# Up-projection of a fused encoder layer by seven block products, with the down-projection as a stage of its own

## The chip, the cores and the metric

One core of a Trainium2 chip runs the whole program. The metric is the device time of one execution in microseconds (us): the median of the runs. TensorE (PE) does the matmuls, VectorE (DVE), ScalarE (ACT) and GpSimd (POOL) work on tiles in the on-chip memory, SyncE (SP) starts most transfers. Matmuls accumulate in PSUM, in eight banks.

## What is computed

One step of an encoder layer on T = 1088 positions (1024 of a new stream, 64 of a running one), D = 1024 channels, float32. Cut to what matters here:

```python
hn = rmsnorm(x, g_pre1)
z = hn @ w_in
# ... gated linear recurrence (ya) and chunk-wise position mixing (yb) ...
mix = jnp.concatenate([ya, yb], axis=-1) @ w_o
x = x + rmsnorm(mix, g_post1)
hn2 = rmsnorm(x, g_pre2)
up = hn2 @ w_up
upc, new_ffn = causal_dwconv(up, ffn_prev, w_conv_f, b_conv_f)
f = (jax.nn.gelu(upc[..., :D_FF]) * upc[..., D_FF:]) @ w_down
x = x + rmsnorm(f, g_post2)
```

w_up is 1024 x 6144 (D_FF = 3072, a gate half and a value half), w_down 3072 x 1024. The convolution is over positions, three taps per channel.

## The kernel before, in words

All activations lie transposed: channels on the 128 partitions, positions along the row. A float32 matmul is done as three matmuls of a reduced format (fp32r): each operand is split into a high part (ScalarE copy, L122) and the rest (VectorE subtraction, L124 or L126), and high x high, high x low and low x high are added up in PSUM. So every product below counts three times.

The stages in order: the v projection (L268, L274), the tiles of the remaining input projection with the position mixing and the recurrence between them (L408, L489), the output projection `o_mm` (L626) in three chunks of positions (364, 364, 360), the code after it for each chunk, `post1`, then the up-projection with the down-projection between its parts, and the tail.

`post1` of a chunk runs beside the matmuls of the next one, piece by piece, as a generator that `o_mm` and `pre_up` step forward. It makes two norms. For each, `rstd_head` puts the sum of squares through TensorE (`st`, L179), VectorE (`v`, L170) and GpSimd (`rs`, a power, L171); `rstd_tail` spreads the result over the partitions with TensorE (`bp`, L191) and ScalarE copies it (`rr`, L193). Between them stand scaling (L682), residual addition (L683) and, in `add_sq`, squares on ScalarE (L201) and their sum (L202), which is on GpSimd for the first norm and for six of eight tiles of the second.

The up-projection has 24 pairs of tiles, a gate tile and a value tile of 128 channels each. The first two pairs (`pre_up`, L737) run chunk by chunk beside the last `post1`. Each other tile is `up_mm` (L721): 8 input tiles, 3 matmuls, 3 chunks, 72 matmuls. ScalarE copies the result out of PSUM (L725), VectorE convolves it in three passes (L762, L765), ScalarE applies GELU (L773), VectorE multiplies gate and value (L779) and the product is split into `gh` and `gl`. After every fourth pair `down` (L804) multiplies four finished pairs with their part of w_down, 288 matmuls, and adds to `facc` (L825, L827). The last group runs in column blocks of 284, 272, 272 and 260 (`last_down`) with the final norm between them.

What each engine does next is an order fixed when the program is built: instructions are queued as the code emits them, with `high_priority` moving a few ahead, and each engine takes its own queue in that order. Weights come by `prefetch`, one or two 512 KB loads ahead on SyncE, and are split when they are there. All larger tiles share one pool of 41 buffers (`NBIG`).

Of the kernel before, what the change touches and what calls it, by code (L numbers as in the profile page):

```python
# [18 lines left out]
GAP = 3  # L19
T = SEQ + DEC  # L20
# [11 lines left out]

LAST_COLS = [(0, 284), (284, 556), (556, 828), (828, 1088)]
LAST_ENG = ["gg", "vv", "vv", "gg", "vv", "vv", "vg", "vv"]
Y_STEPS = [(0,), (0, 0), (1, ), (2,), (1,), (1, 2), (2,), ()]
NPRE = 2
PRI = 120
NBIG = 41
# [17 lines left out]
def layer_kernel(ctx: ExitStack, tc, xT, w_fm, w_v, w_o, w_up, w_down, w_g, w_s, par, bc, yT, small, vn_out):  # L56
# [3 lines left out]
    quad = ctx.enter_context(tc.tile_pool(name="quad", bufs=1))  # L60
# [10 lines left out]
    def big_tile(dt=F32, shape=(P, 3 * CH), name="t"):  # L71
        return big.tile(list(shape), dt, tag="t", name=name)

    def tmp_tile(w, name="d"):
        return tmp.tile([P, NSB * P], F32, tag="d", name=name)[:, :w]

    def quad_tile(name):
        return quad.tile([P, 4, 3 * CH], F32, tag="q", name=name)
# [6 lines left out]

    def third(i, c):
        return slice(i % 3 * CH, i % 3 * CH + cw(c))
# [8 lines left out]
    def packed(n, dt, name, c):  # L96
        tiles = [big_tile(dt, name=name) for _ in range((n + 2) // 3)]
        return [tiles[i // 3][:, third(i, c)] for i in range(n)], tiles

    def v3(t, n, c):  # L100
        return t.rearrange("p (c t) -> p c t", c=3)[:, :n, :cw(c)]
# [30 lines left out]
    w_src.update({("up", i): w_up[i] for i in range(2 * NF)})  # L132
# [3 lines left out]
    for j in range(NF):  # L136
        order += [("up", 2 * j), ("up", 2 * j + 1)]
        if j % GRP == 0 and j:
            order += [("dn", j // GRP - 1, m) for m in range(4)]
    order += [("dn", NF // GRP - 1, m) for m in range(4)]  # L140
# [3 lines left out]
    shut = {"up"}  # L144
# [178 lines left out]
    s = quad_tile("s")  # L323
# [38 lines left out]
    def v_gate(b):  # L362
# [5 lines left out]
        for h in range(4):  # L368
            nc.vector.scalar_tensor_tensor(s[:, h, vcols(b)], sp[:, h, :n], pv("g_v", h), cc[:, h, :n],
                                           op0=ALU.mult, op1=ALU.add)  # L370
# [30 lines left out]
    def fm_mm(w, evac, fill=(), by_chunk=False):  # L401
        fill = list(fill)
        ps = [bank_tile("ps") for _ in range(3)]
        hi, lo = w

        def one(k, q, c):
            wt, at = ((hi, xh), (hi, xl), (lo, xh))[q]
            nc.tensor.matmul(ps[c][:, :cw(c)], wt[:, k * P:(k + 1) * P], at[k][:, cs(c)],  # L408
                             start=(k == 0 and q == 0), stop=(k == KD - 1 and q == 2))

        if by_chunk:
            for c in range(3):
                for k in range(KD):
                    for q in range(3):
                        one(k, q, c)
                evac(c, ps[c][:, :cw(c)])
        else:
            for k in range(KD):
                for q in range(3):
                    for c in range(3):  # L420
                        one(k, q, c)
# [6 lines left out]
            for c in range(3):  # L428
                evac(c, ps[c][:, :cw(c)])
# [86 lines left out]
    def u_tile(h, fill=()):  # L516
        sh = s[:, h, :T]
# [18 lines left out]
    def gate_tile_chunks(t, after):  # L536
# [3 lines left out]
        def evac(c, ps):  # L540
            nc.vector.tensor_tensor(g[:, cs(c)], ps, rb[c], op=ALU.mult)
            nc.scalar.activation(g[:, cs(c)], g[:, cs(c)], AF.Gelu_apprx_tanh)
            nc.vector.tensor_tensor(h[:, cs(c)], h[:, cs(c)], g[:, cs(c)], op=ALU.mult)
            sat3[c] = tmp_tile(cw(c), name="sat3")
            nc.scalar.activation(sat3[c], h[:, cs(c)], AF.Square)
            after(c)
# [20 lines left out]
    def slots(n, name):  # L567
        tiles = [None] * ((n + 2) // 3)

        def at(i, c):  # L570
            if tiles[i // 3] is None:
                tiles[i // 3] = big_tile(F32R, name=name)
            return tiles[i // 3][:, third(i, c)]

        return at

    yh, yl = {}, {}
    ysl = [slots(24, "yha"), slots(24, "yhb")]

    def y_split(c, half):  # L580
        head = rstd_head((sat if half == 0 else sbt)[:, cs(c)], DA, None if half else sat3[c])
        yield
        rr = tmp_tile(cw(c), name="rr")
        rstd_tail(head, rr)
        for i in range(4):
            k = half * 4 + i
            y = (hst[i] if half == 0 else s[:, i, :])[:, cs(c)]
            nc.vector.scalar_tensor_tensor(y, y, pv("g_out", k), rr, op0=ALU.mult, op1=ALU.mult)
            yh[k, c], yl[k, c] = ysl[half](c * 8 + 2 * i, c), ysl[half](c * 8 + 2 * i + 1, c)
# [12 lines left out]
    ys = [y_split(c, 1) for c in range(3)]  # L602
    for t in range(3):
        step(ys[t])
        gate_tile(t, [None, None, None, None, lambda: step(ys[t]), None, lambda: step(ys[t])])
    ys = [y_split(c, 0) for c in range(3)]
    gate_tile_chunks(3, lambda c: None)

# [3 lines left out]
    def o_mm(c, gen=iter(())):  # L612
        pss = {}

        def half_mm(mp, half, mi, first, last):
# [6 lines left out]
            ps = pss[m][:, :cw(c)]  # L622
            for i in range(4):
                k = half * 4 + i
                for j, (w, a) in enumerate(((hi, yh), (hi, yl), (lo, yh))):
                    nc.tensor.matmul(ps, w[:, i * 256 + mi * P:i * 256 + (mi + 1) * P], a[k, c],  # L626
                                     start=(first and i == 0 and j == 0), stop=(last and i == 3 and j == 2))

        if c == 1:
            q = quad_tile("mixq")  # L630
            mix = [q[:, i // 3, third(i, c)] for i in range(9)]
        else:
            mix, _ = packed(9, F32, "mix", c)
        ssq = mix.pop()

        def evac(m):
            nc.scalar.activation(mix[m], pss[m][:, :cw(c)], AF.Copy)
            add_sq(ssq, mix[m], m == 0, nc.gpsimd)

        if c == 0:  # L640
            for n, (mp, half) in enumerate(O_ORDER):
# [4 lines left out]
                for mi in range(2):  # L646
                    half_mm(mp, half, mi, half == 1, half == 0)
                    if half == 0:
                        evac(2 * mp + mi)
        else:  # L650
            for m in range(KD):
# [4 lines left out]
                if c == 2 and m % 2 == 1:  # L656
                    del wo[0, m // 2], wo[1, m // 2]
                    if m == 3:
                        shut.clear()
# [345 lines left out]
```

## Time and profile before

| what | value |
|---|---|
| time, median of 3 runs | 1251.18 us (1249.62 to 1251.53) |
| profiled execution: span from first to last instruction | 1244.9 us |
| median less that span | 6.3 us |
| TensorE busy, mean granted clock | 97%, 0.987 |
| VectorE, ScalarE, GpSimd busy | 53%, 32%, 11% |
| transferred | 75.50 MB, mean 61 GB/s |

The profile is of one execution of its own; the page gives its span, and the time around it is taken as the difference to the median. A share of busy time is a mean over stages with different limits, so a stage is read by itself: with the chain that ended last, the waits, and windows of the span. In the chain's lines "x24" counts the instructions of the piece; for statistics and broadcasts each matmul of the program shows as two there.

### The profile page before, as it was taken

The numbers are of one execution on the slowest core, as the hardware profiler recorded it, in microseconds if no ns is written. First come the engines' busy times: TensorE is split into PE (matmuls) and PEld (weight loads), VectorE is DVE, ScalarE is ACT, GpSimd is POOL, SyncE is SP. The second block draws the span as 40 slices with busy tenths as digits, with TensorE's granted clock in tenths as the row PEclk, the third lists the DMA queues.
The fourth block names the chain that finished last, engine by engine and source line by source line (L and its number), as shares of the span: only waits on it lengthen the run. The fifth ranks groups of instructions, "written<-read, shape, count | busy, mean of one in ns | idle before, by whom it ended". The sixth has DMA issues, their size and how long they took to land.

```text
span 1244.9 us, 17414 instructions
## 1 busy us (share of the span) xinstructions
PE 1210.9 (97%) x7334; PEld 1193.9 (96%) x7334; DVE 664.1 (53%) x958; ACT 392.5 (32%) x663; POOL 135.3 (11%) x233
## 2 busy tenths in 40 slices
PE   8998999998899999999999999999999999999995
PEld 6798999998899999999999999999999999999995
DVE  7585777655676755025542545425453353534676
ACT  7214656453443324222320222112320222112332
POOL 0213000034431000000000000000000000000045
PEclk9999999999998999999999999999999999999998
DMA  8110111211341112011111111211111111211323
GB/s 294 34 39 18 34 52 34 103 48 49 120 161 48 68 34 67 19 52 34 35 62 40 34 35 51 69 35 35 51 52 51 35 34 35 68 51 35 115 88 107
DMA packets 31421, 75.50 MB, mean 61 GB/s; under 512 B 2640, under 2 KB 17488, under 8 KB 31344
## 3 DMA queue, kind: packets, MB, share of 16 engines
q1 hardware_dynamic: 30672, 73.76, 17.7%
q8 instruction: 57, 0.93, 0.3%
q10 hardware_dynamic: 624, 0.53, 0.1%
q14 instruction: 20, 0.16, 0.0%
q0 software_dynamic: 48, 0.11, 0.0%
HBM read 65.24 MB, written 9.16 MB: 60 GB/s over the span
## 4 chain that ended last, share of the span: by engine, by line
PE 90%; DVE 6%; issue 2%; ACT 1%; DMA 0%; SPq 0%; POOL 0%; ACTq 0%; DVEq 0%
PE ups L721 42%; PE dps L804 19%; PE ps L408 11%; PE ops L626 6%; PE vps L274 3%; PE pps L737 3%; PE lps L804 2%; PE gps L489 1%; DVE xs L683 1%; DVE mix L682 1%; PE st L179 1%; DVE xc L473 1%; PE bp L191 1%; PE sp L366 1%; DVE mixq L682 0%
## 5 line engine op out<-in xcount | busy, mean ns | idle before, releaser
L721 PE MATMUL ups<-hhl,whi 128*128 128x364 f32 (+1 forms) x2112 | 407.0, 328 | 0.0
L721 PEld LDWEIGHTS ups<-hhl,whi 128*128 128x128 f32 x2112 | 357.3, 188 | 0.0
L721 PE MATMUL ups<-hhl,wlo 128*128 128x364 f32 (+1 forms) x1056 | 232.1, 328 | 0.0
L721 PEld LDWEIGHTS ups<-hhl,wlo 128*128 128x128 f32 x1056 | 182.8, 188 | 0.0
L124 DVE TENSOR_TENSOR wlo<-wraw,whi 128x1024 fp32r<-128x1024 f32 x96 | 116.6, 1219 | 77.2 <-ACT whi L122 41.5
L725 ACT ACTIVATE uraw<-ups 128x364 f32<-128x364 f32 (+2 forms) x176 | 55.7, 403 | 257.7 <-PE ups L721 257.7
L122 ACT ACTIVATE whi<-wraw 128x1024 fp32r<-128x1024 f32 x96 | 101.0, 1059 | 103.5 <-DVE wlo L124 101.0
L804 PE MATMUL dps<-gh,whi 128*128 128x364 f32 (+1 forms) x480 | 105.5, 328 | 0.0
L804 PE MATMUL dps<-gh,wlo 128*128 128x364 f32 (+1 forms) x480 | 105.5, 328 | 0.0
L762 DVE TENSOR_SCALAR yv<-uraw,pt 128x1091 f32<-128x1091 f32 (+3 forms) x27 | 21.1, 785 | 158.0 <-ACT uraw L725 157.7
L804 PE MATMUL dps<-gl,whi 128*128 128x364 f32 (+1 forms) x480 | 105.3, 327 | 0.0
L757 POOL COPY sm<-uraw 128x2 f32<-128x2 f32 x48 | 10.2, 213 | 777.5 <-ACT uraw L725 750.0
L804 PEld LDWEIGHTS dps<-gl,whi 128*128 128x128 f32 x480 | 83.1, 188 | 0.0
L804 PEld LDWEIGHTS dps<-gh,whi 128*128 128x128 f32 x480 | 83.0, 188 | 0.0
L804 PEld LDWEIGHTS dps<-gh,wlo 128*128 128x128 f32 x480 | 82.9, 188 | 0.0
L762 DVE TENSOR_SCALAR yg<-uraw,pt 128x1091 f32<-128x1091 f32 x24 | 20.3, 848 | 111.5 <-ACT uraw L725 107.6
L408 PE MATMUL ps<-xh,whi 128*128 128x364 f32 (+1 forms) x288 | 67.8, 332 | 0.0
L765 DVE SCALAR_TENSOR_TENSOR yv<-uraw,pt,yv 128x1090 f32<-128x1090 f32 (+5 forms) x54 | 66.0, 1227 | 1.6
L408 PE MATMUL ps<-xh,wlo 128*128 128x364 f32 (+1 forms) x288 | 66.2, 328 | 0.0
L408 PE MATMUL ps<-xl,whi 128*128 128x364 f32 (+1 forms) x288 | 66.1, 328 | 0.0
L765 DVE SCALAR_TENSOR_TENSOR yg<-uraw,pt,yg 128x1090 f32<-128x1090 f32 (+1 forms) x48 | 64.8, 1351 | 0.8
L122 ACT ACTIVATE gh<-yp 128x1088 fp32r<-128x1088 f32 (+3 forms) x27 | 27.3, 1013 | 111.2 <-DVE yp L779 111.2
(225 smaller groups left out, 1752.2 us busy)
## 6 DMA issues: line engine op xcount, KB each, us to landing
wraw<-in_w_up_dram SPq DMA_DIRECT2D x48, 512.0 KB, 3.5
wraw<-in_w_down_dram SPq DMA_DIRECT2D x24, 512.0 KB, 3.4
wraw<-in_w_fm_dram SPq DMA_DIRECT2D x12, 512.0 KB, 3.5
wraw<-in_w_o_dram SPq DMA_DIRECT2D x8, 512.0 KB, 3.5
xr<-in_xT_dram SPq DMA_DIRECT2D x7, 544.0 KB, 9.7
xs<-in_xT_dram SPq DMA_DIRECT2D x4, 546.0 KB, 3.9
xd<-xs SPq DMA_DIRECT2D x4, 546.0 KB, 3.2
xn<-xd SPq DMA_DIRECT2D x4, 408.0 KB, 6.4
```

The costliest lines, as they stand in the source:

```text
L122: nc.scalar.activation(hi, src, AF.Copy, scale=1.0 if scale is None else scale)
L124: nc.vector.tensor_tensor(lo, src, hi.bitcast(F32), op=ALU.subtract)
L179: nc.tensor.matmul(st[:sb, b:b + 1], ssq[:, o:o + sb], ones[:, 0:1], start=True, stop=more is None)
L274: nc.tensor.matmul(ps[b][:vrows(b), :], a[:, vcols(b)], wt[:, o:o + 512], start=False, stop=(k == KD - 1 and q == 2))
L408: nc.tensor.matmul(ps[c][:, :cw(c)], wt[:, k * P:(k + 1) * P], at[k][:, cs(c)], start=(k == 0 and q == 0), stop=(k == KD - 1 and q == 2))
L626: nc.tensor.matmul(ps, w[:, i * 256 + mi * P:i * 256 + (mi + 1) * P], a[k, c], start=(first and i == 0 and j == 0), stop=(last and i == 3 ...
L721: nc.tensor.matmul(ps[c], w[:, k * P:(k + 1) * P], a[k, c], start=(k == 0 and j == 0), stop=(k == KD - 1 and j == 2))
L725: nc.scalar.activation(raw[:, g], ps[c][:, d], AF.Copy)
L737: nc.tensor.matmul(ps, wt[:, k * P:(k + 1) * P], a[k, c], start=(k == 0 and j == 0), stop=(k == KD - 1 and j == 2))
L762: nc.vector.tensor_scalar(y[:, lo:hi], x[:, lo:hi], tap(2), pv("b_conv_f", i), op0=ALU.mult, op1=ALU.add)
L765: nc.vector.scalar_tensor_tensor(y[:, o:hi], x[:, o - d:hi - d], tap(2 - d), y[:, o:hi], op0=ALU.mult, op1=ALU.add)
L804: nc.tensor.matmul(dst, wt[:, i * 256 + mi * P:i * 256 + (mi + 1) * P], at, start=(i == 0 and q == 0), stop=(last and q == 2))
```

## The change

The up-projection of pairs 2 to 23 is done by one level of Strassen's scheme in Winograd's form. The weight of a pair is a 2 x 2 block matrix (gate and value channels by the two halves of the 1024 inputs: A11, A12, A21, A22), the activations another (halves of the inputs by even and odd chunks of 274 positions: B11, B12, B21, B22). Eight block products become seven, of sums and differences of blocks: four weight combinations S1 to S4 for each pair, made by VectorE and split (`operands`), and four activation combinations T1 to T4, made once in `post1` and kept. Partial sums stay in PSUM banks while ScalarE and VectorE take intermediate states out of them (`copy`, `add`). The seventh product of a pair is issued after the first of the next pair (`late`).

The gated product `yg` of each pair is written to DRAM (`gd`) and read back (`load_g`) by the down-projection, which now starts when all up-products are done; its five groups and the last one are as before. The first tap of the convolution moves from VectorE to ScalarE. Output projection, `post1`, the first two pairs and the last gate tile go by four chunks of positions (274, 274, 274, 266) in place of three, and the sums of squares of the output projection and of `post1` move from GpSimd to VectorE. The pool of large buffers grows to 47, without the four-tile buffer that stood beside it.

```diff
-    order += [("dn", NF // GRP - 1, m) for m in range(4)]
+    order += [("up", i) for i in range(2 * NPRE)]
+    order += [("dn", g, m) for g in range(NF // GRP) for m in range(4)]
...
-            add_sq(ssq, mix[m], m == 0, nc.gpsimd)
+            add_sq(ssq, mix[m], m == 0)
...
-            add_sq(ss2, xm(m), m == 0, nc.gpsimd if m < 6 else nc.vector)
+            add_sq(ss2, xs[m], m == 0)
...
+        if c % 2 == 1:
+            (b11, b21), (b12, b22) = hn.pop(c - 1), hn.pop(c)
+            for name, out, p, q in (("T1", b11, b12, b11), ("T3", b12, b22, b12), ("T2", b22, b22, b11),
+                                    ("T4", b21, b21, b22)):
+                nc.vector.tensor_tensor(out, p, q, op=ALU.subtract)
+                split_b(name, c // 2, out)
+                yield
...
-        nc.vector.tensor_scalar(y[:, lo:hi], x[:, lo:hi], tap(2), pv("b_conv_f", i), op0=ALU.mult, op1=ALU.add)
+        nc.scalar.activation(y[:, :TG], x[:, :TG], AF.Identity, scale=tap(2), bias=pv("b_conv_f", i))
...
+        nc.vector.tensor_tensor(yg[:, :TG], yg[:, :TG], yv[:, :TG], op=ALU.mult)
+        for g, d in PIECES:
+            nc.sync.dma_start(gd[j][:, d], yg[:, g])
...
+PRODUCTS = [("B11", "A11"), ("T2", "S2"), ("B21", "A12"), ("T3", "S3"), ("T1", "S1"), ("T4", "A22"), ("B22", "S4")]
...
+        yield op(a11)
+        nc.vector.tensor_tensor(s1, a21, a22, op=ALU.add)
+        sub(s2, s1, a11)
+        yield op(s2)
+        yield op(a12)
+        sub(s3, a11, a21)
+        yield op(s3)
+        yield op(s1)
+        yield op(a22)
+        sub(s4, a12, s2)
+        yield op(s4)
...
+        for c in range(2):
+            bh, bl = opb[b, c]
+            for k in range(4):
+                for q, (wt, at) in enumerate(((hi, bh), (hi, bl), (lo, bh))):
+                    nc.tensor.matmul(dst[c], wt[:, k * P:(k + 1) * P], at[:, fourth(k)],
...
+        product(j, 0, main, True)
+        copy(q1, main)
+        if late:
+            late.pop()()
+        tick()
+        product(j, 1, main, False)
+        copy(q2, main)
+        tick()
+        b0 = [bank_tile("up0")[:, :QW] for _ in range(2)]
+        product(j, 2, b0, True)
+        add(q1, b0, q1)
+        tick()
+        product(j, 3, main, False)
+        copy(q4, main)
+        b2 = [bank_tile("up2")[:, :QW] for _ in range(2)]
+        product(j, 4, b2, True)
+        add(q4, b2, q4)
+        product(j, 5, main, False)
+        copy(q3, main)
+
+        def last():
+            product(j, 6, b2, False)
+            add(q2, b2, q2)
+            todo.append(gated(j, xg, xv))
...
+    def load_g(j):
+        raw = big_tile(name="graw")[:, :T]
+        nc.sync.dma_start(raw, gd[j])
+        gg[j] = big_tile(F32R, name="gh")[:, :T], big_tile(F32R, name="gl")[:, :T]
+        split(*gg[j], raw)
...
+    shut.clear()
+    for j in range(GRP):
+        load_g(j)
+    prefetch()
+    while todo:
+        run(todo.pop(0))
-    nc.gpsimd.dma_start(small, sm)
+    nc.sync.dma_start(small, sm)
+    for g in range(NG - 1):
```

Three places in the order of the engines follow.

TensorE, in the output projection of the last chunk, at the statistics (`st`) and broadcast (`bp`) of the second norm in `post1`. Before, for the second chunk (sixteen rows of `ops`, 24 matmuls, lie between):

```order
L626 MATMUL ops<-yha,wlo 128x360
L179 MATMUL st<-ones,xs 122x1 x3
L626 MATMUL ops<-yhb,whi 128x360 x2
L626 MATMUL ops<-yhb,wlo 128x360
...
L626 MATMUL ops<-yha,wlo 128x360
L191 MATMUL bp<-ident,rs 128x122 x2
L191 MATMUL bp<-ident,rs 128x120
```

After, for the third of four chunks:

```order
L634 MATMUL ops<-yh,whi 128x266
L188 MATMUL st<-ones,ss_3325 92x1 x3
L634 MATMUL ops<-yl,whi 128x266
L634 MATMUL ops<-yh,wlo 128x266
L634 MATMUL ops<-yh,whi 128x266
L634 MATMUL ops<-yl,whi 128x266
L200 MATMUL bp<-ident,rs 128x92 x2
L200 MATMUL bp<-ident,rs 128x90
```

Four matmuls stand there now between the statistics and the broadcast that needs them; the last chunk's two norms, among the `pps` matmuls, show the same.

VectorE, in the up-projection, the work of one tile pair. Before (`uraw` is a tile out of PSUM, `yg` and `yv` the convolved gate and value tile, `yp` their product, `wlo` and `gl` low parts); these rows are a whole pair:

```order
L755 COPY uraw<-pt 128x3
L762 TENSOR_SCALAR yg<-uraw,pt 128x1091
L765 SCALAR_TENSOR_TENSOR yg<-uraw,pt,yg 128x1090
L124 TENSOR_TENSOR wlo<-wraw,whi 128x1024
L765 SCALAR_TENSOR_TENSOR yg<-uraw,pt,yg 128x1089
L755 COPY uraw<-pt 128x3
L762 TENSOR_SCALAR yv<-uraw,pt 128x1091
L765 SCALAR_TENSOR_TENSOR yv<-uraw,pt,yv 128x1090
L765 SCALAR_TENSOR_TENSOR yv<-uraw,pt,yv 128x1089
L779 TENSOR_TENSOR yp<-yg,yv 128x1024
L779 TENSOR_TENSOR yp<-yg,yv 128x64
L124 TENSOR_TENSOR gl<-yp,gh 128x1088
```

After, half of a pair (`wsum` is a combination S, `wop` the low part of an operand; numbers after `up` tell PSUM banks apart):

```order
L780 SCALAR_TENSOR_TENSOR yv<-uraw,pt,yv 128x1089
L877 TENSOR_TENSOR uraw<-up_8784,uraw 128x274
L795 TENSOR_TENSOR yg<-yg,yv 128x1091
L877 TENSOR_TENSOR uraw<-up_8785,uraw 128x274
L816 TENSOR_TENSOR wsum<-wraw 128x512
L771 COPY uraw<-pt 128x3
L814 TENSOR_TENSOR wsum<-wsum,wraw 128x512
L136 TENSOR_TENSOR wop<-wsum,wop 128x512
L136 TENSOR_TENSOR wop<-wraw,wop 128x512
L814 TENSOR_TENSOR wsum<-wraw 128x512
L877 TENSOR_TENSOR uraw<-up_8850,uraw 128x274
```

Additions out of PSUM, which free banks, now stand between the operand work and the convolution in one queue; the first tap and the split of the gated product are gone from it.

ScalarE, where the first group of the down-projection begins. Before, the first copy of its results (`fq<-dps`) stood right behind the copies of an up tile:

```order
L725 ACTIVATE uraw<-ups 128x364 x2
L725 ACTIVATE uraw<-ups 128x296
L725 ACTIVATE uraw<-ups 128x64
L825 ACTIVATE fq<-dps 128x364
L122 ACTIVATE gh<-yp 128x1088
```

After, behind the last copy out of the up-products' banks (two more `gh`, three more `whi` and the taps of the last pair lie in the gaps):

```order
L872 ACTIVATE uraw_9151<-up1_9153 128x274
L134 ACTIVATE gh_9402<-graw_9400 128x1088
...
L134 ACTIVATE whi_9422<-wraw_9418 128x1024
...
L778 ACTIVATE yg_9447<-uraw_8915,pt_79 128x1091
L778 ACTIVATE yv_9455<-uraw_8916,pt_79 128x1091
...
L789 ACTIVATE yg_9447<-yg_9447 128x1091
L134 ACTIVATE gh_9483<-graw_9481 128x1088
L789 ACTIVATE yg_9465<-yg_9465 128x1091
L953 ACTIVATE facc_9526<-dps_9487 128x364
```

The splits of the first down operands and the rest of the last two pairs (taps L778, GELU L789) stand ahead of the first copy of a down result.

## Rows read from the trace of the kernel before

**Rows 1.** The page: span, busy time by engine, and the chain's shares.

```profile
span 1244.9 us, 17414 instructions
PE 1210.9 (97%) x7334; PEld 1193.9 (96%) x7334; DVE 664.1 (53%) x958; ACT 392.5 (32%) x663; POOL 135.3 (11%) x233
PE 90%; DVE 6%; issue 2%; ACT 1%; DMA 0%; SPq 0%; POOL 0%; ACTq 0%; DVEq 0%
```

**Rows 2.** Chain that ended last (start us, us, what), up and down stage.

```profile
412.76 71.56 PE ups L721 x432
484.31 47.64 PE dps L804 x288
531.96 95.44 PE ups L721 x576
```

**Rows 3.** TensorE's waits: who was waited for, us, times, longest.

```profile
PE st L179 <- DVE xs L202: 10.1, 3, 4.0
```

**Rows 4.** The chain: two pieces behind a wait, and one that is not (320.47).

```profile
301.46 5.64 PE ops L626 x24
...
320.47 4.06 PE ops L626 x24
...
381.78 6.58 PE pps L737 x24
```

**Rows 5.** Windows: span, busy PE, PEld, DVE, ACT, POOL; then clock, DMA share, GB/s.

```profile
301.40:307.10 5.70, 5.70 (x27) 5.70 (x27) 0.16 (x1) 0.00 (x0) 1.80 (x2) 0.70 0.00 0
307.80:312.00 4.20, 4.20 (x27) 4.20 (x26) 3.46 (x7) 2.45 (x6) 0.97 (x1) 1.00 0.02 4
...
412.00:1176.00 764.00, 764.00 (x4613) 764.00 (x4612) 339.62 (x407) 178.22 (x309) 13.86 (x88) 1.00 0.14 45
```

**Rows 6.** TensorE's timeline (start us, us) in the last stage: first and last of 48.

```profile
1198.82 0.29 PE L804 MATMUL lps<-gh,whi 128*128 128x272 f32 x1
...
1204.69 0.29 PE L804 MATMUL lps<-gh,wlo 128*128 128x272 f32 x1
```

**Rows 7.** The chain, first piece of the last down stage.

```profile
1176.18 15.59 PE lps L804 x120
```

**Rows 8.** Groups by line and shape: busy us, mean ns of one, idle before.

```profile
L124 DVE TENSOR_TENSOR wlo<-wraw,whi 128x1024 fp32r<-128x1024 f32 x96 | 116.6, 1219 | 77.2 <-ACT whi L122 41.5 <-issue 35.5
L765 DVE SCALAR_TENSOR_TENSOR yg<-uraw,pt,yg 128x1090 f32<-128x1090 f32 x24 | 32.5, 1354 | 0.8
L893 DVE TENSOR_TENSOR facc<-lps,facc 128x272 f32<-128x272 f32 x8 | 3.4, 428 | 0.0
L122 ACT ACTIVATE whi<-wraw 128x1024 fp32r<-128x1024 f32 x96 | 101.0, 1059 | 103.5 <-DVE wlo L124 101.0 <-DMA wraw<-in_w_up_dram 2.1 <-DVE sat L210 0.4
L773 ACT ACTIVATE yg<-yg 128x1091 f32<-128x1091 f32 x24 | 26.8, 1117 | 88.7 <-DVE yg L765 54.0 <-DVE uraw L755 34.6
L498 ACT ACTIVATE r<-r,s 128x1088 f32<-128x1088 f32 x4 | 4.8, 1207 | 0.1
L825 ACT ACTIVATE facc<-dps 128x364 f32<-128x364 f32 x8 | 3.4, 472 | 18.1 <-PE dps L804 18.1
```

**Rows 9.** Transfers: issues, KB each, median us from issue to landing.

```profile
wraw<-in_w_up_dram SPq DMA_DIRECT2D x48, 512.0 KB, 3.5
...
xd<-xs SPq DMA_DIRECT2D x4, 546.0 KB, 3.2
```

**Rows 10.** The chain, one set of statistics and one of broadcasts.

```profile
279.61 0.54 PE st L179 x6
...
307.10 0.66 PE bp L191 x6
```

**Rows 11.** VectorE's timeline (start us, us) in post1 of the first chunk.

```profile
288.12 1.10 DVE L682 SCALAR_TENSOR_TENSOR mix<-mix,pt,rr 128x364 f32<-128x364 f32 x2
...
290.03 2.54 DVE L682 SCALAR_TENSOR_TENSOR mix<-mix,pt,rr 128x364 f32<-128x364 f32 x2
```

**Rows 12.** GpSimd's timeline in the same stretch.

```profile
288.82 3.35 POOL L202 TENSOR_TENSOR xs<-xs,sq 128x364 f32<-128x364 f32 x2 [2.42 <-ACT sq L201]
```

More of the change, by code (lines that the diff above doesn't have):

```diff
@@ L649, in o_mm @@
                         evac(2 * mp + mi)
+            for g in ys:
+                run(g)
         else:
@@ L711, in layer_kernel @@
[L711 to L726 removed]
+            f = tiles[m // 4][:, fourth(m)]
@@ new lines, in post1 @@
+        hn[c] = tiles
+        if c % 2 == 1:
[4 more added lines that the diff above has]
+                split_b(name, c // 2, out)
+                yield
+    gen = iter(())
+    for c in range(4):
+        o = o_mm(c, gen)
+        run(gen)
+        gen = post1(c, *o)
@@ new lines, in layer_kernel, with start_ops, fetch_ops @@
+    opgen = {}
+    opq = []
+    opnext = [(NPRE, 0)]
+    for j in range(NPRE, NF):
+        opnext += [(j, i) for i in range(1, 6)] + [(j + 1, 0)] * (j + 1 < NF) + [(j, 6)]
+    def start_ops(j):
+        if j < NF and j not in opgen:
+            opgen[j] = operands(j)
+            next(opgen[j])
+    def fetch_ops(n):
+        while len(opq) < n and opnext:
+            j, i = opnext.pop(0)
+            if i == 0:
+                start_ops(j)
+            if i == 3:
+                start_ops(j + 1)
+            opq.append(next(opgen[j]))
@@ new lines, in layer_kernel, with product @@
+    late = []
+    todo = []
+    def product(j, i, dst, start):
+        fetch_ops(1)
+        hi, lo = opq.pop(0)
+        b = PRODUCTS[i][0]
+        for c in range(2):
+            bh, bl = opb[b, c]
+            for k in range(4):
+                for q, (wt, at) in enumerate(((hi, bh), (hi, bl), (lo, bh))):
+                    nc.tensor.matmul(dst[c], wt[:, k * P:(k + 1) * P], at[:, fourth(k)],
+                                     start=(start and k == 0 and q == 0), stop=(k == 3 and q == 2),
+                                     skip_group_check=True)
+        fetch_ops(OP_AHEAD)
@@ new lines, in up_pair, with copy, add, tick @@
+    def up_pair(j):
+        xg, xv = big_tile(name="uraw"), big_tile(name="uraw")
+        q1, q2, q3, q4 = ([x[:, fourth(2 * c + r)] for c in range(2)]
+                          for x, r in ((xg, 0), (xg, 1), (xv, 0), (xv, 1)))
+        main = [bank_tile("up1")[:, :QW] for _ in range(2)]
+        def copy(dst, src):
+            for c in range(2):
+                with tc.high_priority(offset=PRI):
+                    nc.scalar.activation(dst[c], src[c], AF.Copy)
+        def add(dst, src, p):
+            for c in range(2):
+                with tc.high_priority(offset=PRI):
+                    nc.vector.tensor_tensor(dst[c], src[c], p[c], op=ALU.add)
+        def tick():
+            if todo:
+                if next(todo[0], 0) == 0:
+                    todo.pop(0)
+        product(j, 0, main, True)
[21 more added lines that the diff above has]
+            todo.append(gated(j, xg, xv))
+        late.append(last)
@@ new lines, in layer_kernel @@
+    start_ops(NPRE)
+    raw = pre_up(2 * NPRE, gen)
+    for j in range(NPRE):
+        todo.append(gated(j, raw[2 * j], raw[2 * j + 1]))
+    fetch_ops(OP_AHEAD)
+    for j in range(NPRE, NF):
+        up_pair(j)
+        while len(todo) > 1:
+            run(todo.pop(0))
+    late.pop()()
+    opb.clear()
+    facc = [None] * KD
+    gg = {}
+    def load_g(j):
[3 more added lines that the diff above has]
+        split(*gg[j], raw)
@@ L918, in layer_kernel @@
     NG = NF // GRP
[L919 to L921 removed]
+    shut.clear()
[3 more added lines that the diff above has]
+    while todo:
+        run(todo.pop(0))
+    nc.sync.dma_start(small, sm)
+    for g in range(NG - 1):
+        if g == NG - 2:
             ahead[0] = 4
[L923 to L926 removed]
+        down(g)
     last_down(NG - 1)
```

304 lines of the change are left out of this document (142 added, 162 removed).

## The prediction

> **What bounds the kernel now.** I read the page's totals first: TensorE is busy 97% of a 1244.9 us span and holds 90% of the chain that ended last, VectorE has 53%, ScalarE 32% [rows 1]. In the chain in order of time the reader is to see that from 412.76 to 1176.18 us nothing but matmuls stands there: six pieces of the up-projection (L721) and, between them, five of 288 matmuls of the down-projection (L804) [rows 2]. The first two up pieces are 71.56 us for 432 matmuls and 95.44 us for 576; both give 165.7 ns a matmul, and so do all 3168 (525.0 us in all). So in that stretch only the number and width of matmuls counts, as long as the other engines keep up. Before it, the post-norm and residual code of the output projection (post1) makes TensorE wait: the list of waits puts 10.1 us in three waits on VectorE's sums of squares [rows 3]. The three pieces behind these waits show more: 24 matmuls take from 5.64 to 6.58 us there, against 4.06 elsewhere in the same stage [rows 4], and the granted clock is 0.70 in the first of them (1.2 GHz for part of it) and 1.00 right after [rows 5]. The waits (10.1), the slow pieces (5.64 + 5.87 + 6.58 - 3 x 4.0 = 6.1; the second is not shown) and issue gaps and stretched statistics matmuls (about 2.3) lose some 18.5 us.
>
> The profiled span is 1244.9 us; the median of the runs is 1251.18, so I carry 6.3 us around the span unchanged.
>
> **The up-projection, the main term.** For 22 of the 24 pairs the eight quarter products become seven: 22 x 7 x 24 = 3696 matmuls of 274 columns, in place of 3168 of 364, 364 and 360. What does one of 274 cost? The trace has none, but the last down stage has neighbours on both sides: 47 steps between the first and last row shown, at 272 columns, take 1204.69 - 1198.82 = 5.87 us, 124.9 ns each; the 120 at 284 take 15.59 us, 129.9 ns [rows 6, 7]. On the line between them 274 is 125.7 ns; those two are the bounds. 3696 x 0.1257 = 464.6 us, against 525.0: **-60.4 us** (-63.4 to -44.9). Total columns say the same: 7/8 of the work, and 0.8% padding.
>
> Is the line straight? From 363 columns to 272 the pitch falls to 0.754 for 0.750 of the columns, so a matmul in a long stream costs its columns and little else [rows 2, 6]. The Trainium skill speaks against this change here: its page "TensorE: Matmul & The Clock Gate", section "Back-to-back issue gap", gives sustained spacings of about 81 ns at 128 columns and 131 at 512, since each matmul brings its weight load; an estimate from that page lets 274 columns cost 90% of 363, and by it the sum would be some 84 us higher, a loss. No row here goes that way; I take the rows.
>
> **Does anything else bound the new pair?** TensorE's pair lasts 168 x 0.1257 = 21.1 us. VectorE per pair: four operand sums and seven splits of 512 columns (half of 1.22 us, 0.61 each: 6.7), six adds of 274 out of PSUM (0.43 as at 272: 2.6), four convolution steps (1.35: 5.4; the first tap has gone to ScalarE), one product (about 1.2) and two small copies (0.3): 16.2 us, 77%. ScalarE: seven splits (half of 1.06: 3.7), eight PSUM copies (0.40, less than the 0.47 of 364 columns: 3.2), two taps (no row; 1.21 like the scaled pass of L498 over as many columns, and not under GELU's 1.12: 2.4), GELU 1.12: 10.4 us [rows 8]. Both fit. What stalls TensorE would be a hand-over: product 1 accumulates on banks that ScalarE must first have copied, but the late product of the pair before stands between, and products 2, 4 and so on likewise: 24 matmuls, 3.0 us, against two copies of 0.40. Operands are made up to five products ahead. The weights still come as two 512 KB loads a pair at 3.5 us, and the gated result adds two writes like the 2.6 to 3.2 us of the residual's (0.55 MB) [rows 9]; on SyncE's queue the next pair's loads stand ahead of those writes. With the DMA share at 0.14 in that stage [rows 5] I cost the up stage's waits at **0**; what hides them is the 3.0 us of each product between.
>
> **Output projection, first pairs, last gate tile in four chunks.** pps 384 x 0.1257 = 48.3 against 288 of 364 (47.7); ops 576 x 0.1257 + 192 x 0.122 = 95.8 against 95.4; the gate tile 0.1: **+1.2**. A fourth chunk brings four more heads: eight sets of statistics (st) and broadcast (bp) matmuls of 0.54 and 0.66 us [rows 10], **+4.8** (3 to 6).
>
> **Post1's waits.** In the trace one pair of VectorE steps takes 1.10 us alone and 2.54 us while GpSimd runs its sums of squares beside it [rows 11, 12]. The change puts those sums on VectorE and leaves GpSimd only the small power step there. A chunk's chain is then 8 steps of about 0.45 (0.55 at 364 columns, alone) and 15 of 0.43 (as at 272 [rows 8]), less some overlap 9 to 10 us, plus 2 us from statistics to broadcast; TensorE has 84 matmuls, 10.6 us, beside it. So the long gaps shrink to 0.5 to 1.5 us at each head. But in three places only a few matmuls stand between st and bp (the order rows above), 0.5 us of cover for 1.9 us. I take 7 us of waits in all for the 18.5: **-11.5** (0 to -16).
>
> **The seam between up and down.** Before, a group of down matmuls stood between up pairs and their inputs were long ready. Now the down stage begins when the last product ends. Its first matmuls need whi, which ScalarE makes behind three gh splits of about 1.1 us: ready about 2 us after the end; wlo comes behind two adds and two gl splits on VectorE (1.2 each, like wlo's 1024 columns) and its own 1.2: about 4.4 us after. The two allow six matmuls meanwhile, so some 3.4 us are lost. Then the third output tile needs the banks of the first, whose copy (0.47) stands on ScalarE behind the last GELU; that waits for VectorE, which has four wlo and then seven convolution steps (1.3) and a product ahead: near 17.8 us after the end, while TensorE would have come at 15.3. Another 3.1 + 0.6 us. With a slow clock after a wait of this length [rows 4, 5] **+8** (3.5 to 14).
>
> Stages before the last gate tile, down groups 1 to 4, the last group and the tail keep their matmuls and order: 0.
>
> **Sum:** -60.4 + 1.2 + 4.8 - 11.5 + 8 = -57.9; span 1187.0, time **1193** us.
>
> **Rivals.**
> *ScalarE's queue holds the PSUM banks (slower).* Place: the copy after product 1, which stands behind a GELU; GELU waits for a VectorE step that stands behind an add out of the late product. Priced from that product's first half: 0.43 + 1.35 + 1.12 = 2.9 us, and the copy is wanted 7.5 us after it. The gain is gone when each pair loses 57.9 / 22 = 2.6 us, so this chain would have to take near 9.7 us, or every hand-over (five a pair, two copies and their signals, 1 us) would have to lie bare: 22 x 5 = 110 us, 1303. For it: two in-order queues wait on each other in every pair. Against: 4 us of slack, VectorE 77% full, and GpSimd, which doubles VectorE's steps in post1, is nearly idle in this stage.
> *Short matmuls cost a fixed part (slower).* Each matmul brings a weight load, which could set the pace. The broadcasts of 122 columns, in pieces of six, take 0.110 us each [rows 10]; on a line from there to 165.7 at 363, 274 columns cost 145 ns, 3696 of them 537 us, and the time is 1265. Against it stand the rows at 272 and 284, which are of the same kind as the new ones. This is the page's case above.
> *Post1 and the seam go badly.* VectorE now carries all sums of squares plus T-operand differences; if post1 saves nothing and the seam costs its upper bound: 1193 + 11.5 + 6 = 1211.
> *They go well.* Post1 loses 2.5 us, the seam 3.5: 1184.
> That the change does not do as it says I rule out: the built order holds 3696 matmuls of 274.
>
> **How the numbers follow.** Forecast 0.68, bad post1 and seam 0.15, good 0.10, bare hand-overs 0.04, short matmuls 0.03. Range 1182 to 1216: the good case with the lower matmul bound, and the bad case with part of the upper one; the two slow rivals stay out. 0.2% of this kernel, 2.5 us, is about what its measurement can tell from no change. Faster 0.92, same 0.01, slower 0.07.
>
> **What would show it.** Right: up matmuls near 465 us in all, 125 to 126 ns each; VectorE 75 to 80% and ScalarE about half busy in that stage with no wait of TensorE there; post1's pieces of 24 matmuls at one pace; one gap near 3 us at the first down matmul and one near the third tile. Wrong: gaps before products (rival one), an unchanged length of the up stage with no gaps (rival two), or a granted clock below 1.00 within the up stage.

## The result, and the profile after

The changed kernel takes 1206.68 us (median of 4, 1205.05 to 1207.4) against 1250.4 us before (4 runs, 1247.64 to 1251.53): a ratio of 0.9653, 95% interval 0.964 to 0.9667, or 43.7 us less. Forecast were 1193 us and a range of 1182 to 1216.

The page of the changed kernel, the lines that answer to [rows 1]:

```profile
span 1205.5 us, 19847 instructions
PE 1164.1 (97%) x8228; PEld 1145.2 (95%) x8228; DVE 787.4 (65%) x1305; ACT 504.4 (42%) x848; POOL 149.3 (12%) x204
PE 88%; DVE 6%; issue 3%; POOL 1%; ACT 1%; DMA 1%; SPq 0%; DVEq 0%; ACTq 0%; POOLq 0%
```

TensorE's share is what it was, of a shorter span; VectorE has risen from 53% to 65% and ScalarE from 32% to 42%, because the operand combinations and their splits are theirs. The span is 39.4 us shorter, the median 43.7. The profiled execution of the changed kernel took 1207.26 us, so 1.8 us lie around its span, not 6.3: what I carried around the span was mostly the difference between the profiled execution of before and the median.

The chain that ended last, in order of time (start us, us, what), where it answers to [rows 2, 4, 7, 10]:

```profile
244.15 3.15 PE ops L634 x24
...
354.52 1.80 POOL rs L180
356.37 0.90 PE bp L200 x6
...
412.15 467.27 PE up L858 x3672
...
886.80 7.59 DMA wraw<-in_w_down_dram
894.41 1.07 ACT whi L134
895.50 1.23 DVE wlo L136
...
907.20 228.98 PE dps L936 x1368
1136.17 15.57 PE lps L936 x120
```

The reader is to see one unbroken piece of up matmuls (the last 24 of the 3696 overlap the next rows; they end at 882.46, which makes 470.31 us for all of them), then a stretch of some 25 us in which a weight transfer, ScalarE and VectorE hold the chain, then one piece of down matmuls. Stage by stage against the chain of before, in us:

| stage | before | after | difference | forecast |
|---|---|---|---|---|
| start to first output-projection piece | 239.01 | 244.15 | +5.1 | 0, and some of the sets |
| output projection, post1, first pairs | 173.75 | 168.0 | -5.8 | -5.5 with all sets |
| up matmuls | 525.0 | 470.3 | -54.7 | -60.4 |
| down matmuls of five groups, with the seam | 238.4 | 253.7 | +15.3 | +8 |
| last group and tail | 68.7 | 69.3 | +0.6 | 0 |

TensorE's waits, in answer to [rows 3]:

```profile
PE dps L936 <- ACT whi L134: 8.7, 1, 8.7
PE bp L200 <- POOL rs L180: 6.1, 5, 1.6
...
PE dps L936 <- ACT facc L953: 2.2, 1, 2.2
PE bp L387 <- DVE cst L350: 1.1, 1, 1.1
```

The three waits for VectorE's sums (10.1 us) are gone, none of the up stage is in the list, and there are three new places: the seam (8.7 and 2.2), the broadcasts behind only a few matmuls (four of the five waits for GpSimd, 4.9 us; the fifth, 1.2 us, is the last group's and stands in the list of before too) and, early, a broadcast that waits for the gate constants (`cst`, 1.1). Windows of the up stage, the seam and the down stage (span, busy PE, PEld, DVE, ACT, POOL; then clock, DMA share, GB/s), beside [rows 5]:

```profile
412.10:879.50 467.40, 467.40 (x3675) 467.40 (x3674) 340.09 (x517) 220.13 (x392) 66.26 (x88) 1.00 0.22 76
879.50:907.20 27.70, 16.83 (x97) 16.31 (x95) 20.04 (x19) 16.09 (x17) 1.42 (x2) 0.82 0.46 163
907.20:1136.20 229.00, 229.00 (x1370) 228.65 (x1371) 94.13 (x136) 49.43 (x62) 0.00 (x0) 0.99 0.34 112
```

In the up stage TensorE is never idle and the granted clock is 1.00 (2.4 GHz); VectorE is busy 73% there, 15.5 us a pair. The seam has 10.9 us of idle TensorE, and the clock 0.82 shows that the matmuls behind the waits ran partly at 1.2 GHz. Its start, TensorE's timeline, shows it row by row:

```profile
891.16 1.27 PE L936 MATMUL dps<-gh,whi 128*128 128x364 f32 x3 [8.70 <-ACT whi L134]
892.23 1.11 PE L936 MATMUL dps<-gl,whi 128*128 128x364 f32 x3
...
895.45 0.67 PE L936 MATMUL dps<-gh,wlo 128*128 128x364 f32 x3
895.95 0.66 PE L936 MATMUL dps<-gh,whi 128*128 128x364 f32 x3
```

Three matmuls take 1.07 us from start to start at first and 0.50 four us later. What the first of them waited for is on SyncE's timeline:

```profile
870.63 1.71 SPq L928 DMA_DIRECT2D graw<-gd  x3
884.45 0.34 SPq L1053 DMA_DIRECT2D out_dram<-sm  x1
884.88 0.38 SPq L928 DMA_DIRECT2D graw<-gd  x1
885.35 2.36 SPq L162 DMA_DIRECT2D wraw<-in_w_down_dram  x5
```

Three reloads go out at 870.63. Then the queue stands until 884.45, at the transfer of the small outputs (`out_dram<-sm`, L1053), which needs the last GpSimd copy of the last pair (L774, 883.13 to 884.4); the fourth reload and five weight loads of the down-projection come behind it. The changed line `nc.sync.dma_start(small, sm)` stood in the diff, a queue away from where it was before.

### The profile page after: what moved, and what is told of

Same layout as the page of the kernel before. It is cut to its first block, busy times and chain, and to the rows that moved or that the text cites. A ratio compares the mean times of both kernels' runs of the same rounds, so it can differ in the third digit from the quotient of the medians.

```text
span 1205.5 us, 19847 instructions
## 1 busy us (share of the span) xinstructions
PE 1164.1 (97%) x8228; PEld 1145.2 (95%) x8228; DVE 787.4 (65%) x1305; ACT 504.4 (42%) x848; POOL 149.3 (12%) x204
## 4 chain that ended last, share of the span: by engine, by line
PE 88%; DVE 6%; issue 3%; POOL 1%; ACT 1%; DMA 1%; SPq 0%; DVEq 0%; ACTq 0%; POOLq 0%
PE up L858 39%; PE dps L936 19%; PE ps L419 11%; PE ops L634 6%; PE pps L750 4%; PE vps L283 3%; PE lps L936 2%; PE gps L500 1%; PE bp L200 1%; DVE facc L974 1%; PE st L188 1%; PE sp L375 1%; DMA wraw<-in_w_down_dram 1%; POOL rs L180 1%; DVE xc L484 1%
## 5 line engine op out<-in xcount | busy, mean ns | idle before, releaser
L858 PE MATMUL up<-bh,wop 128*128 128x274 f32 x2464 | 470.5, 290 | 0.0
L858 PEld LDWEIGHTS up<-bh,wop 128*128 128x128 f32 x2464 | 389.3, 189 | 0.0
L858 PE MATMUL up<-bl,wop 128*128 128x274 f32 x1232 | 356.6, 289 | 0.0
L858 PEld LDWEIGHTS up<-bl,wop 128*128 128x128 f32 x1232 | 233.3, 189 | 0.0
L936 PE MATMUL dps<-gh,whi 128*128 128x364 f32 (+1 forms) x480 | 107.4, 332 | 10.9 <-ACT whi L134 8.7
L872 ACT ACTIVATE uraw<-up 128x274 f32<-128x274 f32 x176 | 68.9, 392 | 114.8 <-PE up L858 114.8
L136 DVE TENSOR_TENSOR wlo<-wraw,whi 128x1024 fp32r<-128x1024 f32 x52 | 63.0, 1218 | 39.6 <-ACT whi L134 30.6
L634 PE MATMUL ops<-yh,whi 128*128 128x274 f32 (+1 forms) x256 | 75.4, 295 | 0.0
L634 PE MATMUL ops<-yl,whi 128*128 128x274 f32 (+1 forms) x256 | 74.0, 289 | 0.0
L634 PE MATMUL ops<-yh,wlo 128*128 128x274 f32 (+1 forms) x256 | 74.0, 289 | 0.0
L136 DVE TENSOR_TENSOR wop<-wsum,wop 128x512 fp32r<-128x512 f32 x88 | 60.2, 686 | 16.4 <-ACT wop L134 16.2
```

The costliest lines, as they stand in the source:

```text
L136: nc.vector.tensor_tensor(lo, src, hi.bitcast(F32), op=ALU.subtract)
L634: nc.tensor.matmul(ps, wt[:, i * 256 + mi * P:i * 256 + (mi + 1) * P], a[k, c], start=(first and i == 0 and j == 0), stop=(last and i == 3 ...
L858: nc.tensor.matmul(dst[c], wt[:, k * P:(k + 1) * P], at[:, fourth(k)], start=(start and k == 0 and q == 0), stop=(k == 3 and q == 2), skip ...
L872: nc.scalar.activation(dst[c], src[c], AF.Copy)
L936: nc.tensor.matmul(dst, wt[:, i * 256 + mi * P:i * 256 + (mi + 1) * P], gg[j0 + i][p][:, cols], start=(i == 0 and q == 0), stop=(last and ...
```

## The experiments

Times are medians of 4 runs each; "ratio" is to the kernel before on the same chip, with its 95% interval.

### The small outputs' transfer back on GpSimd's queue

```diff
-    nc.sync.dma_start(small, sm)
+    nc.gpsimd.dma_start(small, sm)
```

> The changed kernel with the transfer of the small outputs on GpSimd's queue again (as before the change) instead of SyncE's. My theory: on SyncE's queue this transfer waited for the last copies of the up-stage and held up the last reload of a gated tile and five weight loads of the down-projection behind it; without it TensorE's 8.70 us wait at the first down matmul shrinks to 2 to 3 us, and with the slow matmuls after it the time falls by 6 to 9 us, to 1198 to 1201 us. Rival: the loads are bound by their buffers or by transfers of one another, or ScalarE's and VectorE's queues are the later wait anyway; then the wait stays over 6 us and the time over 1204 us.

1201.16 us, ratio 0.9609 (0.9584 to 0.9634), 5.5 us less than the changed kernel. TensorE's waits at the first down matmuls are now

```profile
PE dps L936 <- DVE wlo L136: 1.7, 1, 1.7
PE dps L936 <- ACT whi L134: 1.4, 1, 1.4
```

in place of the 8.7 for `whi`. From the start of the up matmuls to the first piece of the last down group the chain has 717.3 us instead of 724.0. So the queue was the cause of most of the wait. The gain is a little under the expected: behind the transfer there were the waits that the prediction had counted. Without it the five groups with the seam take 247.0 us, 8.6 more than before, against a forecast of 8.

### The gate constants back between the normalisations

```diff
         if k == 3:
-            gate_const()
+            with tc.high_priority(offset=16):
+                gate_const()
```

> The changed kernel with the four VectorE steps that make the gate constants moved from behind the second three normalisations to between the first and second three, where they stood before the change. My theory: they hold a PSUM bank that the second broadcast of the input norm needs, so this move made TensorE's whole work after 55 us start about 4.5 us later; undone, the wait of 1.1 us at that broadcast goes and the first matmul of the output projection starts 3 to 4.5 us earlier, time 1202 to 1204 us. Rival: the later start comes from the earlier statistics of the input norm and not from this, and the time stays at 1206 to 1207 us.

1203.6 us, ratio 0.9637 (0.9618 to 0.9655): about 3 us less by the medians, 2 by the ratios, whose intervals overlap. TensorE's timeline of the changed kernel and then of this one, at the second broadcast of the input norm, each with VectorE's row of the gate constants:

```profile
59.22 1.13 PE L387 MATMUL bp<-ident,rt 128*128 128x128 f32 x8 [1.11 <-DVE cst L350]
57.95 1.12 DVE L350 SCALAR_TENSOR_TENSOR cst<-wsum,pt,bw 128x128 f32<-128x128 f32 x4
```

```profile
57.56 1.05 PE L387 MATMUL bp<-ident,rt 128*128 128x128 f32 x8
53.88 1.12 DVE L350 SCALAR_TENSOR_TENSOR cst<-wsum,pt,bw 128x128 f32<-128x128 f32 x4
```

The wait is gone and the output projection starts at 241.99 instead of 244.15, about half of the shift that I expected. Single executions differ there, but the two groups do not meet: in the seven profiles with the constants behind (the changed kernel and six of its variants) it starts between 243.46 and 245.29, in the five with them moved between 241.99 and 242.54. So the move is worth about 2 us. Most of the other 3 us of the table's 5.1 is probably not the change's: the kernel before with another part edited far behind this place (the VectorE sums, below) starts its output projection at 241.11, 2.1 us later than the profiled execution of before.

### Both

> Both of these edits together. My theory: they lie in different stages and add up, 10 to 13 us, so 1194 to 1197 us. Rival: one hides the other or neither is worth it, over 1200 us.

1198.3 us, ratio 0.9591 (0.9571 to 0.9611): 8.4 us, about the sum of 5.5 and 3.1. It missed the expected 1194 to 1197 by a little, as its parts did. TensorE's waits at the seam are now those of the prediction's working:

```profile
PE dps L937 <- DVE wlo L136: 1.7, 1, 1.7
...
PE dps L937 <- ACT whi L134: 1.4, 1, 1.4
PE dps L937 <- ACT facc L954: 1.3, 1, 1.3
```

whi first, then wlo, then the bank of the first result behind the last GELU. Counted from the end of the up matmuls (882.12), the first matmul with wlo starts 4.3 us later and the last GELU is done 17.6 us later, where the prediction had 4.4 and 17.8. Three matmuls take 0.60 us from start to start after the first wait and 1.07 after the second, against 0.50 at full clock.

### Six products instead of seven

```diff
         def last():
-            product(j, 6, b2, False)
+            fetch_ops(1)
+            opq.pop(0)
+            fetch_ops(OP_AHEAD)
             add(q2, b2, q2)
```

> The changed kernel without the seventh product of each of the 22 pairs (its 24 matmuls are left out, its operands are still made; the value part of the up-projection is then incomplete). My theory: the up stage is bound by TensorE alone, 127.2 ns a matmul of 274 columns, so 22 x 24 x 0.1272 = 67 us go, time 1139 to 1142 us. Rival: VectorE (16 to 17 us of work a pair against the 18.3 us that are left to TensorE) or hand-overs of banks bind close to the present pace; then less than 50 us go and waits of TensorE show in that stage.

1138.49 us, ratio 0.9113 (0.9095 to 0.9131): 68.2 us less, against 22 x 24 x 127.2 ns = 67.2. The window from 412 to 810 us:

```profile
412.00:810.00 398.00, 398.00 (x3128) 398.00 (x3128) 335.46 (x514) 213.73 (x388) 31.69 (x88) 1.00 0.24 85
```

TensorE is busy all 398 us and VectorE 335. So with 18.3 us a pair, too, the stage is TensorE's alone, and one product is worth its 24 matmuls.

### More work for VectorE

```diff
         nc.vector.tensor_tensor(yg[:, :TG], yg[:, :TG], yv[:, :TG], op=ALU.mult)
+        for _ in range(3):
+            nc.vector.scalar_tensor_tensor(yv[:, :TG], yv[:, :TG], 1.0, yg[:, :TG], op0=ALU.mult, op1=ALU.mult)
```

> The changed kernel with three useless VectorE passes of 1.35 us over each pair's gated product (4.05 us a pair; the outputs stay the same). VectorE's 15.5 us a pair become 19.6 of TensorE's 21.4. My theory: VectorE has slack and operands are made ahead, so the up stage stays as long; the tail of the last two pairs at the seam grows by some of the 4 to 8 us added there; time 1207 to 1213 us. Rival: hand-overs of PSUM banks and operands are already close, and each pair loses part of the 4 us: over 1225 us.

1209.19 us, ratio 0.9679 (0.9664 to 0.9694): 2.5 us more, none of it in the up stage (467.48 us for the same 3672 matmuls). With six passes:

> The same with six passes, 8.1 us a pair: 23.6 us of VectorE against 21.4. My theory: VectorE now sets the pace, 2.2 us more a pair, 48 us over 22 pairs, and 5 to 15 at the seam: 1255 to 1272 us. Rival (VectorE's order of work is elastic or its rows overlap more than I count): under 1240 us.

1234.88 us, ratio 0.9886 (0.987 to 0.9903): 28 us more, not the 48 and more I had expected. Windows from 420 to 860 us, three passes and then six:

```profile
420.00:860.00 440.00, 440.00 (x3458) 440.00 (x3457) 396.29 (x561) 204.56 (x370) 74.44 (x82) 1.00 0.22 75
```

```profile
420.00:860.00 440.00, 422.13 (x3286) 418.39 (x3285) 435.43 (x581) 192.22 (x347) 137.64 (x76) 1.00 0.21 72
```

At 90% VectorE costs TensorE nothing; at 99% it is the bound, and 3286 matmuls fit where 3458 did. The bound is at a full engine, as my theory had it, but the price was too high. One pass and the row after it on VectorE:

```profile
607.54 1.28 DVE L797 SCALAR_TENSOR_TENSOR yv<-yv,yg 128x1091 f32<-128x1091 f32 x1
608.74 0.78 DVE L879 TENSOR_TENSOR uraw<-up,uraw 128x274 f32<-128x274 f32 x2
```

A pass lasts 1.28 us, not 1.35, and the next row starts 1.20 us after it does, so six cost 7.2 us, not 8.1; a pair came to 22.5 us instead of 23.6. By number the rival's line (under 1240) was met, and its reason, rows that overlap more than I had counted, is part of why.

### The sums of squares, on both kernels

On the kernel before, this part of the change alone:

```diff
-            add_sq(ssq, mix[m], m == 0, nc.gpsimd)
+            add_sq(ssq, mix[m], m == 0)
...
-            add_sq(ss2, xm(m), m == 0, nc.gpsimd if m < 6 else nc.vector)
+            add_sq(ss2, xm(m), m == 0)
```

> The kernel before with one part of the change alone: the sums of squares of the output projection and of the norms after it on VectorE instead of GpSimd. My theory: VectorE's steps there, stretched to twice their length by GpSimd's work on the same stretch, run at their own pace; TensorE's three waits (10.1 us) fall below 5 us and some of the slow matmuls behind them go, 6 to 12 us in all, 1238 to 1244 us. Rival: the eight more sums on VectorE take what the others save, time 1247 to 1251 us.

1231.23 us, ratio 0.9854 (0.9839 to 0.987): 18.2 us less, more than I expected. Windows of the stage from 240 to 412 us, before and with this edit:

```profile
240.00:412.00 172.00, 161.87 (x970) 160.64 (x969) 106.48 (x159) 72.97 (x146) 55.83 (x51) 0.95 0.25 84
```

```profile
240.00:412.00 172.00, 172.00 (x1081) 171.65 (x1081) 116.40 (x211) 78.72 (x157) 11.79 (x19) 1.00 0.27 94
```

TensorE has no idle time left there, the granted clock is 1.00 instead of 0.95, and the up stage starts at 397.01 instead of 412.76. On the changed kernel the same lines set back to GpSimd:

> The changed kernel with this part alone undone: the sums of squares on GpSimd. My theory: the waits of TensorE for VectorE's sums come back, 6 to 12 us, 1213 to 1219 us. Rival: the four narrower chunks are what removed the waits; time stays at 1205 to 1209 us.

1226.06 us, ratio 0.9818 (0.9798 to 0.9838): 19.4 us more, and the list of waits has VectorE's sums again:

```profile
PE st L188 <- DVE ss L211: 11.5, 4, 3.8
```

So the engine of the sums decides, not the width of the chunks. Both expectations were too small: they counted the 10.1 us of waits and only some of what stands behind them, while the 18.5 us of the prediction also had 6.1 of matmuls at the lower clock (0.94 in this run's window, 0.95 before) and 2.3 of issue gaps and stretched statistics. It follows that the sums' move, which needs no block products, is 18 of the 43.7 us; the rest of the change is worth 24 (1250.4 to 1226.06 with the sums on GpSimd, 1231.23 to 1206.68 with them on VectorE).

### Two columns less

```diff
-                    nc.tensor.matmul(dst[c], wt[:, k * P:(k + 1) * P], at[:, fourth(k)],
+                    n = QW if k == 0 and q == 0 else 272
+                    nc.tensor.matmul(dst[c][:, :n], wt[:, k * P:(k + 1) * P], at[:, fourth(k, n)],
```

> The changed kernel with 11 of 12 up matmuls two columns narrower (272 of 274; the last two columns of each chunk are then incomplete). My theory: a matmul costs its columns, 125.0 ns at 272 against 127.2 at 274, so 3388 x 2.2 ns = 7.5 us go, 1198 to 1201 us. Rival: at two columns less the pitch falls by 0.9 ns only (0.44 ns a column, the slope between 272 and 364) and the rest of the 127.2 comes from other work beside the stream: 3 us go, 1203 to 1205 us.

1203.27 us, ratio 0.9629 (0.9615 to 0.9644): 3.4 us less. The chain's up piece, and the first and last of 71 matmuls of 272 columns in a row in this run's last down stage (start us, us):

```profile
413.86 465.46 PE up L859 x3684
```

```profile
1152.76 0.28 PE L937 MATMUL lps<-gl,whi 128*128 128x272 f32 x1
...
1161.54 0.28 PE L937 MATMUL lps<-gh,wlo 128*128 128x272 f32 x1
```

The rival holds: two columns are worth 1 ns. Less the 307 that kept 274 columns, the up stage has 126.3 ns a matmul at 272; the last down stage has 8.78 / 70 = 125.4 here, and had 124.9 in the execution of before.

### The seam in another order

On top of both edits; the lines are those against the changed kernel, and the gate constants are moved as above.

```diff
-    for j in range(GRP):
+    load_g(0)
+    ahead[0], n0 = 0, ahead[0]
+    prefetch()
+    ahead[0] = n0
+    for j in range(1, GRP):
         load_g(j)
-    prefetch()
-    while todo:
-        run(todo.pop(0))
-    nc.sync.dma_start(small, sm)
...
         down(g)
+        while todo:
+            run(todo.pop(0))
+        if g == 0:
+            nc.gpsimd.dma_start(small, sm)
```

> On top of both edits: at the seam the first down weight is loaded and split right behind the first gated tile, and the rest of the last two pairs (convolution, GELU, product) is issued behind the first group of the down-projection instead of ahead of it. My theory: the three waits left at the seam (1.4 for whi, 1.7 for wlo, 1.3 for the bank of the first result) and the slow matmuls behind them go, 4 to 6 us, time 1192 to 1195 us. Rival: the four reloads of gated tiles and the weight loads share one queue and land too late, so the wait only changes its name; time stays at 1197 to 1199 us.

1195.17 us, ratio 0.9564 (0.9547 to 0.9581): 3.1 us less than both edits, just outside the expected. The first down matmul follows the last up matmul at 882.47 without a gap, and the first group runs 286 matmuls in 47.49 us. A new wait stands behind it:

```profile
PE dps L937 <- DVE facc L956: 3.2, 1, 3.2
```

VectorE's first sum of the second group stands behind the two pairs' convolution steps, which now come in a row there (the rest of the last two pairs). With one pair behind the first group and one behind the second (`if todo: run(todo.pop(0))` in place of the loop, the small outputs behind the second):

> The seam variant with the rest of the last two pairs split up: one pair behind the first group of the down-projection, the other behind the second. My theory: TensorE's wait of 3.2 us for VectorE's first sum of the second group, which stood behind eight convolution steps and two products in a row, goes with the slow matmuls behind it, 3 to 5 us, time 1190 to 1193 us. Rival: half the steps still stand ahead of that sum and are late enough; time 1194 to 1196 us.

1191.01 us, ratio 0.9527 (0.9511 to 0.9543). The chain's down stage is one piece:

```profile
882.06 238.92 PE dps L937 x1440
1120.98 15.61 PE lps L937 x120
```

This is the fastest version of the study, 58.6 us under the kernel before and 15.7 under the changed one, with the same arithmetic.

### The broadcasts later

```diff
-        rstd_tail(head, rr2)
+        with tc.high_priority(offset=-120):
+            rstd_tail(head, rr2)
```

The same at `rr`; both on top of the first seam variant.

> On top of that: in the norms after the output projection the broadcast matmuls are given a lower priority, so that 17 to 98 matmuls, not 4, stand between statistics and broadcast on TensorE. My theory: the five waits of TensorE for GpSimd's power step (6.1 us) go, 4 to 6 us. Rival: VectorE's chain of scaling, adding and squaring sets the pace of that stage; with the broadcast later the chain starts later, the next statistics wait for VectorE instead, and the time stays or rises by up to 5 us.

1201.25 us, ratio 0.9613 (0.9597 to 0.9629): 6.1 us more than that variant. The rival was right, and its 5 us were passed. The up stage starts at 416.53 instead of 412.16, and TensorE waits at the first pairs' weights (1.7 for `whi`, 0.7 for `wlo`) and in one long wait for GpSimd's power step (3.1 instead of 4.9 in four; the last group's 1.2 stands in both). A broadcast delayed delays VectorE's chain behind it, which ends the stage: in the chain that ended last, the last broadcast (397.16) is followed by VectorE's scaling (13 steps from 397.87) and splits up to 406.02, while without this edit TensorE holds 92% of the chain from 380 us to the up stage.

## Why the prediction held, and where it was off

**The up-projection.** Right in kind: no wait, clock 1.00, one product worth 24 matmuls. The term was mis-sized: 470.3 us, not 464.6, because a matmul of 274 columns takes 127.2 ns in the long stream, 1.5 more than the prediction's line between 272 and 284. A small part of that was a misread row: of the 120 matmuls in 15.59 us only 96 have 284 columns (32 for each of three pairs of operands),

```profile
L804 PE MATMUL lps<-gh,whi 128*128 128x284 f32 x32 | 9.4, 294 | 0.0
```

and the other 24 have 272. Without those (24 x 0.125 = 3.0 us) one of 284 takes 131.1 ns, and the line gives 125.9 at 274. The larger part is that both neighbours were rows of the last down stage of one execution: in the run with two columns less, the up stage is 0.9 ns slower at 272 columns than the last down stage of the same execution, and that stage is 0.5 ns slower than in the execution of before. What makes the stages differ stays open. VectorE's load is not it: with three more passes a pair, VectorE 90% busy, a matmul takes 127.3 ns, in the run with six products the same, and in the output projection, whose VectorE work differs, 84 take 10.69 us, 127.3 each. The estimate that the prediction made from the Trainium skill ("TensorE: Matmul & The Clock Gate", "Back-to-back issue gap") did not hold here: 274 columns cost 0.77 of 363, not 0.90.

**Nothing else bounds the pair.** Right. Worked out were 16.2 and 10.4 us of VectorE and ScalarE a pair, measured 15.5 and 10.0 (340 and 220 us over 22 pairs). The runs with extra passes place the point where VectorE decides between 90% and 99%.

**Four chunks and post1.** Right, nearly term by term: -5.8 us measured from the first output-projection piece, where +1.2, +4.8 and -11.5 (18.5 lost before, less 7 of waits that stay) were summed. The move of the sums alone takes 17.9 us out of that stage of the kernel before (173.75 to 155.9), nearly all of the 18.5. The changed kernel's 168.0 is 12.1 above those 155.9: 2.8 are matmuls (at 127.2 ns; forecast 1.2), 4.9 the four waits for GpSimd's power step, which the prediction had named ("only a few matmuls stand between st and bp") and counted with others at 7, and the 4.4 left are near the 4.8 for the sets of the fourth chunk. The others, 0.5 to 1.5 us at each head, did not come. That the misses of 1.6 and 2.1 cancel is luck. No run changes the number of chunks alone, so this split of the 12.1 is worked out and not shown.

**The seam.** The step that failed. I worked it out from ScalarE's and VectorE's queues, and the run with both edits shows these waits where I put them. But I took the weights as loaded: "on SyncE's queue the next pair's loads stand ahead of those writes" was said of the up stage, and the small outputs' transfer that the diff moves onto this queue was not followed to what stands behind it. It cost 5.5 us. The seam came to 15.3 instead of 8, and to 8.6 without the transfer on this queue.

**Stages before the last gate tile: 0.** Wrong by 2 to 3 us. TensorE's order there is nearly the same, but VectorE's had the gate constants three normalisations later, and they free the bank that the next broadcast needs. The lines of code that make them are the same in both kernels; which part of the change moved them in the order, no run shows. I compared one engine's order and not the other's.

**The time around the span.** I carried 6.3 us; it is 1.8. The profiled execution of before was some 4.5 us faster than the median. That error (-4.5 on my side) hid a quarter of the others: the span was forecast at 1187.0 and came to 1205.5, 18.5 more: 5.7 up matmuls, 7.3 seam, 2 to 3 gate constants, about 2 the early execution of before, 0.6 the tail. That it did is luck.

**The rivals.** Bare hand-overs and a fixed part of short matmuls are excluded by the run with six products and by the pitch. "Post1 and the seam go badly" was half right, in the seam alone: 1211 was its number, 1206.7 the time.

## What to carry to other kernels

A saving in matmuls is worth its columns where TensorE is never idle; check with one product left out. A transfer that moves to another queue is costed by what stands behind it there: one small store that waits for the last copy of a stage held up six loads of the next. When a stage ends at once instead of being interleaved, put what the next stage needs first ahead of the leftovers of the last on every queue, and spread the leftovers: here that was worth 7.3 us (1198.3 to 1191.0).

## What the runs showed of the hardware

Two things I had not expected. First, the price of GpSimd and VectorE adding side by side: [rows 11] showed a doubling of two steps, but moving 36 sums (12 a chunk) from one engine to the other in a stretch of 170 us gave 18 us, because, beside the 10.1 us of waits it caused, every wait was followed by matmuls at 1.2 GHz: the clock of the window went from 0.95 to 1.00. Second, the pitch of matmuls of one width is not quite the same in two stages of one execution, 126.3 ns in the up stage against 125.4 in the last down stage at 272 columns, and 124.9 there in another execution; 0.9 ns on 3696 matmuls is 3 us.
